# A convolution with max pooling: row sums with one operand in PSUM, head casts on ScalarE, and a new instruction order

## Chip, core and metric

One Trainium2 chip; the kernel runs on one of its cores. The metric is the device time of one execution in microseconds, the lower the better. The five engines of the core are called as in the profile: PE (TensorE; PEld is its loading of weights), DVE (VectorE), ACT (ScalarE), POOL (GpSimd) and SP (SyncE, which only issues transfers here).

## What is computed

```python
def setup_inputs():
    batch, c_in, h, w, c_out, k = 16, 64, 64, 64, 128, 3
    ...
def reference(x, weight, pool_size):          # pool_size is 2
    x_pad = np.pad(x, ((0, 0), (0, 0), (1, 1), (1, 1)))
    conv[b, co] += weight[co, ci, kh, kw] * x_pad[b, ci, kh:kh+h, kw:kw+w]   # over ci, kh, kw
    output[b, c, i, j] = np.max(conv[b, c, 2*i:2*i+2, 2*j:2*j+2])
```

A 3x3 convolution of 16 images with 64 channels into 128 channels, and the maximum over squares of 2x2. All arrays are float32 in memory; the kernel multiplies in bfloat16.

## The kernel before

Two images lie on the 128 partitions, 64 channels each (half 0 and half 1). Each of the 8 pairs of images is cut into 4 chunks of 16 image rows, so there are 32 pieces, numbered 0 to 31. A piece gives 8 rows of pooled output for each half. A matmul uses 64 rows of the PE array, and the matmuls of half 0 and half 1 run side by side: the function `product` puts the products of each half into a queue of its own (`lanes`) and issues them one from each queue at a time, three taps each, so six matmuls.

The two conv rows that are pooled together share their middle filter row. The kernel therefore computes two accumulators in PSUM for each piece and half (ta and tb), takes their maximum, and adds the common part afterwards. There are two ways to do this, told apart by the letter in `TYPES`:

- K pieces (11 of them) come from `kx`, an array already in bfloat16 (loaded by POOL's queue with a cast on the way, `LK.n.part`; the first two chunks are loaded in float32 and cast by an engine). Products PA1 and PA2 fill ta, PB1 and PB2 fill tb. `EV` (ACT) copies ta to SBUF, `MX` (DVE) takes the maximum into tb, `KS` (DVE) makes the sum of neighbouring rows, PR adds its product to tb, `OD` (ACT) copies the odd columns to SBUF, `CM` (DVE) takes the maximum with the even columns.
- W pieces (21) come from `wx`, three float32 buffers loaded by SP's queue (`L` and `LB`). `E` is the difference of neighbouring rows (on POOL, or on DVE for those in `DIFF_ON_VECTOR`), `D` the difference of rows two apart (POOL), `WS` the sum of neighbouring rows (DVE; for those in `SUM_BY_REDUCTION` as a reduction with one input, else as an addition with two inputs in SBUF). P2 makes ta from E, `SE` (ACT) copies ta into tb, P0 and P3 add the products of D to ta and tb, then EV, MX, P1 (from WS), OD and CM as above.

`MX.s.h` is the maximum of piece s and half h, and so on for all names. The head turns the weights: `g0`, `g1`, `g2` cast filter rows to bfloat16, `D0`, `D2`, `GM`, `GP` combine them (with `GS` on POOL), `T..` transposes on PE, `V..` copies the result to SBUF. `XEa`, `XEb`, `XOa`, `XOb` cast the first chunk (even and odd rows, parts a and b; tile `kfirst`), `X1` and `X2` the second (`ksecond`). `F.k.part` and `G.k.part` are the first K and W pieces' products in halves; `Ea`, `Eb`, `Da`, `Db`, `SEa`, `SEb` the first W piece's other work in halves.

Everything runs in the sequence of the text `ORDER`: each engine takes its own entries in that sequence, waiting for data and for buffers. PSUM has eight banks, handed out from a queue of free ones. One further wait is put in by hand: an operation of POOL waits for the last DVE operation, before it in the text, that was marked with `on_vector` (`on_gpsimd`, `behind`); reductions are not marked. The loads `LB` and the first `LK` wait in the same way. The output of a piece is stored by SP's queue as soon as its second CM stands in the text.

The profile's lines: 200 the products, 301 KS, 315 and 323 the two forms of WS, 332 E, 341 D, 399 and 401 EV, 411 SE, 427 MX, 431 OD, 437 CM, 353 and 368 the first W piece's E and D, 451 the casts of the first chunk, 458 of the second, 175 to 181 the weight copies, 95, 106 and 447 the transfers of kx, wx and the output.

Of the kernel before, what the change touches and what calls it, by code (L numbers as in the profile page):

```python
# [11 lines left out]
def kernel(  # L12
# [169 lines left out]

# [145 lines left out]
    def we(s):  # L328
        row["we", s] = e_pool.tile([128, R, W], BF16, name="we")
        t, f = wx_rows(s)  # L330
        vector = s in DIFF_ON_VECTOR
        inst = (nc.vector if vector else nc.gpsimd).tensor_tensor(  # L332
# [261 lines left out]
```

## Time and profile before

| | |
|---|---|
| time, median of 3 runs | 104.88 us (104.57 to 104.96) |
| profiled execution, span from first to last instruction | 103.4 us |
| the profiled execution's own time | not listed apart; the median lies 1.5 us above the span |
| busy: PE, DVE, ACT, POOL | 96.6, 91.9, 82.1, 75.7 us |
| mean granted clock of TensorE | 0.997 |
| moved by DMA | 23.33 MB, mean 226 GB/s |

All times of events are microseconds from the start of the span. A row of the timeline or of the chain gives start, duration and what ran; a group row gives line, engine, operation, output<-input, count, then busy time, mean ns of one, and the idle time just before with what ended it. The rows of stretches give the sum, then busy time (and count) of PE, PEld, DVE, ACT and POOL, the granted clock, the DMA share and GB/s. PE counts as busy from the first to the last of overlapping matmuls, so a short hole between two matmuls is seen in their starts only.

### The profile page before, as it was taken

What the parts mean: (1) busy time and instruction counts of PE and PEld (TensorE: products, weight loads), DVE (VectorE), ACT (ScalarE), POOL (GpSimd) and SP (SyncE); (2) the same over time, 40 slices, a digit from 0 to 9 for tenths busy, and PEclk for the clock granted to TensorE, in tenths of its full rate; (3) what the DMA queues carried; (4) which work ended last, traced back from release to release, by engine and by line L of the source; (5) the groups of instructions that cost most, each with busy time, mean ns of one, the idle gap of its engine ahead of it and who ended that gap; (6) DMA issues with size and microseconds to landing.
All of it is one profiled execution on the core that took longest, in us unless ns stands there. A gap on an engine that the chain in (4) does not pass through costs nothing.

```text
span 103.4 us, 2542 instructions
## 1 busy us (share of the span) xinstructions
PE 96.6 (93%) x909; PEld 60.1 (58%) x909; DVE 91.9 (89%) x179; ACT 82.1 (79%) x181; POOL 75.7 (73%) x65
## 2 busy tenths in 40 slices
...
GB/s 63 265 297 283 389 319 337 384 405 270 219 212 307 304 302 292 341 356 225 175 131 210 252 381 263 51 203 271 173 158 257 80 136 101 0 13 223 74 202 102
DMA packets 13341, 23.33 MB, mean 226 GB/s; under 512 B 1040, under 2 KB 9488, under 8 KB 13328
## 3 DMA queue, kind: packets, MB, share of 16 engines
...
q0 software_dynamic: 864, 2.36, 13.9%
q8 instruction: 7, 0.11, 0.4%
...
## 4 chain that ended last, share of the span: by engine, by line
PE 83%; DMA 6%; DVE 5%; SPq 1%; issue 1%; DVEq 0%
PE acc L200 83%; DMA wx<-in_x_dram 6%; DVE acc L427 2%; DVE o L437 2%; DVE we L353 1%; SPq L114 0%; SPq L113 0%; SPq L109 0%; DVE ks L301 0%; DVEq L589 0%; DVEq L437 0%
## 5 line engine op out<-in xcount | busy, mean ns | idle before, releaser
L200 PEld LDWEIGHTS <-wt 64*128 64x128 bf16 x876 | 57.7, 94 | 34.1 <-issue 1.6
L341 POOL TENSOR_TENSOR wd<-wx 128x1024 bf16<-128x1024 f32 x20 | 47.1, 2360 | 7.6 <-PE acc L200 2.9
L200 PE MATMUL acc<-kx,wt 64*128 64x504 bf16 (+6 forms) x288 | 50.1, 356 | 0.4 <-DVE wt L181 0.4
L200 PE MATMUL acc<-wd,wt 64*128 64x504 bf16 (+3 forms) x264 | 50.1, 367 | 0.0
L427 DVE TENSOR_TENSOR acc<-acc,ev 128x512 f32<-128x512 f32 x64 | 42.0, 693 | 0.9 <-ACT ev L401 0.3
L200 PE MATMUL acc<-we,wt 64*128 64x512 bf16 (+2 forms) x132 | 31.9, 367 | 0.0
L200 PE MATMUL acc<-ws,wt 64*128 64x504 bf16 (+1 forms) x126 | 28.7, 377 | 0.1
L401 ACT ACTIVATE ev<-acc 128x512 f32<-128x512 f32 x42 | 25.1, 608 | 2.7 <-PE acc L200 2.3
L431 ACT COPY od<-acc 128x256 f32<-128x256 f32 x64 | 22.6, 379 | 5.8 <-PE acc L200 5.2
L437 DVE TENSOR_TENSOR o<-acc,od 128x256 f32<-128x256 f32 x64 | 24.5, 416 | 2.1 <-ACT od L431 1.9
L411 ACT COPY acc<-acc 128x512 f32<-128x512 f32 x40 | 23.0, 581 | 3.0 <-PE acc L200 1.7
L332 POOL TENSOR_TENSOR we<-wx 128x512 bf16<-128x512 f32 x16 | 20.2, 1271 | 3.4 <-DVE ws L323 2.4
L200 PE MATMUL acc<-ks,wt 64*128 64x504 bf16 (+1 forms) x66 | 16.5, 377 | 0.4 <-DVE acc L427 0.4
L315 DVE TENSOR_REDUCE ws<-wx 128x512 bf16<-128x1024 f32 x11 | 13.5, 1230 | 0.0
L399 ACT COPY ev<-acc 128x512 f32<-128x512 f32 x22 | 12.9, 595 | 0.6 <-PE acc L200 0.5
L323 DVE TENSOR_TENSOR ws<-wx 128x512 bf16<-128x512 f32 x10 | 7.0, 720 | 0.0
L301 DVE TENSOR_TENSOR ks<-kx 128x512 bf16<-128x512 bf16 x11 | 4.6, 429 | 0.4 <-ACT kx L458 0.4
L551 PE MATMUL acc<-const-bfloat16-1.0 128*128 128x512 bf16 x8 | 3.3, 589 | 0.8 <-PEq L575 0.8
L95 POOL DMA_DIRECT2D kx<-in_x_dram x6 | 3.5, 587 | 0.7 <-DVE kx L451 0.7
L151 POOL COPY wq<-wq 128x64 bf16<-128x64 bf16 x3 | 0.9, 314 | 3.2 <-ACT wq L462 2.5
L465 DVE TENSOR_TENSOR wq<-wraw 128x192 bf16<-128x192 f32 x1 | 0.5, 498 | 2.6 <-DMA wraw<-in_weight_dram 2.6
L368 POOL TENSOR_TENSOR wd<-wx 128x512 bf16<-128x512 f32 x2 | 2.5, 1260 | 0.4 <-DVE we L353 0.4
...
## 6 DMA issues: line engine op xcount, KB each, us to landing
...
kx<-in_x_dram POOLq DMA_DIRECT2D x1, 496.0 KB, 13.1
```

The lines of the kernel that those rows point to most:

```text
L200: nc.tensor.matmul(acc[t][:, i0:i1, o0:o1], wt[lo : lo + CI, tap_of(m0, kw, h), :], rows(lo, i0, i1, c0, c1), start=start and kw == 1, sto ...
L301: nc.vector.tensor_tensor(out=row["ks", s], in0=t[:, f : f + 2 * R : 2, :], in1=t[:, f + 1 : f + 2 * R : 2, :], op=ADD)
L315: nc.vector.tensor_reduce(out=row["ws", s], in_=t[:, f : f + 2 * R, :].rearrange("p (r two) w -> p r w two", two=2), axis=mybir.AxisListTy ...
L323: nc.vector.tensor_tensor(out=row["ws", s], in0=t[:, f : f + 2 * R : 2, :], in1=t[:, f + 1 : f + 2 * R : 2, :], op=ADD)
L332: inst = (nc.vector if vector else nc.gpsimd).tensor_tensor(out=row["we", s], in0=t[:, f : f + 2 * R : 2, :], in1=t[:, f + 1 : f + 2 * R : ...
L341: nc.gpsimd.tensor_tensor(out=row["wd", s], in0=t[:, f + 1 : f + 1 + 2 * R, :], in1=t[:, f - 1 : f - 1 + 2 * R, :], op=SUB)
L399: nc.scalar.copy(out=ev[s, h], in_=acc[t])
L401: nc.scalar.mul(ev[s, h], acc[t], -1.0)
L411: nc.scalar.copy(out=acc[t], in_=acc[ta[s, h]])
L427: nc.vector.tensor_tensor(out=t, in0=t, in1=ev[s, h], op=MAX)
L431: nc.scalar.copy(out=od[s, h], in_=acc[tb[s, h]][:, :, 1::2])
L437: nc.vector.tensor_tensor(out=ot[s][:, h], in0=acc[t][:, :, 0::2], in1=od[s, h], op=MAX)
```

## The change

- Six row sums (pieces 4, 6, 16, 17, 19, 23) take their odd rows from a PSUM bank, into which ACT copies them first (new entry `XC`); the difference of piece 6, on DVE, reads the same copy. These DVE operations are not marked `on_vector`.
- Seven sums instead of eleven are reductions: 1, 3, 8, 11, 12, 25 and 30.
- The differences on DVE are those of 3, 6, 11 and 27 instead of 3, 4, 6 and 11.
- In the head ACT casts XEa, XOa and XOb (DVE did), DVE casts g0 (ACT did); the weight copies of G2 and G1 are on ACT and the others on DVE (G0, G2 and GM were on ACT).
- The stores are entries of their own (`ST`) and no longer follow their second CM at once.
- Six pools get one to three more buffers.
- `ORDER` is another text. Its first and last lines are shown.

```diff
@@ -35,9 +35,15 @@
 
 
     TYPES = "KWKWWKWKWWKWWKWKWWKWWKWWWWKWWKWW"
-    DIFF_ON_VECTOR = (3, 4, 6, 11,)
+    DIFF_ON_VECTOR = (3, 6, 11, 27,)
     CAST_ON_VECTOR = ()
-    SUM_BY_REDUCTION = (1, 3, 9, 11, 12, 14, 16, 17, 19, 20, 22,)
+    SUM_BY_REDUCTION = (1, 3, 8, 11, 12, 25, 30,)
+    ODD_ROWS_IN_PSUM = (4, 6, 16, 17, 19, 23,)
+    TURNED_BY_SCALAR = ("G2", "G1",)
+    CAST_BY_SCALAR = ("XEa", "XOa", "XOb",)
+    TAPS_BY_VECTOR = ("g0",)
+    SUMS_BY_GPSIMD = ()
+    COLMAX_ON_GPSIMD = ()
     N = len(TYPES)
     KSTEPS = [s for s in range(N) if TYPES[s] == "K"]
     WSTEPS = [s for s in range(N) if TYPES[s] == "W"]
@@ -47,13 +53,13 @@
 
     const = ctx.enter_context(tc.tile_pool(name="const", bufs=1))
     kx_pool = ctx.enter_context(tc.tile_pool(name="kx_pool", bufs=-(-NK // NQ)))
-    d_pool = ctx.enter_context(tc.tile_pool(name="d_pool", bufs=5))
-    e_pool = ctx.enter_context(tc.tile_pool(name="e_pool", bufs=5))
-    ws_pool = ctx.enter_context(tc.tile_pool(name="ws_pool", bufs=5))
+    d_pool = ctx.enter_context(tc.tile_pool(name="d_pool", bufs=8))
+    e_pool = ctx.enter_context(tc.tile_pool(name="e_pool", bufs=7))
+    ws_pool = ctx.enter_context(tc.tile_pool(name="ws_pool", bufs=7))
     ks_pool = ctx.enter_context(tc.tile_pool(name="ks_pool", bufs=4))
-    ev_pool = ctx.enter_context(tc.tile_pool(name="ev_pool", bufs=7))
-    od_pool = ctx.enter_context(tc.tile_pool(name="od_pool", bufs=6))
-    o_pool = ctx.enter_context(tc.tile_pool(name="o_pool", bufs=6))
+    ev_pool = ctx.enter_context(tc.tile_pool(name="ev_pool", bufs=8))
+    od_pool = ctx.enter_context(tc.tile_pool(name="od_pool", bufs=8))
+    o_pool = ctx.enter_context(tc.tile_pool(name="o_pool", bufs=8))
     psum = ctx.enter_context(tc.tile_pool(name="psum", bufs=1, space=bass.MemoryType.PSUM))
 
     ctx.enter_context(tc.manual_schedule())
@@ -171,14 +177,27 @@
         free.append(turned[m])
         lo, hi, src = turned_cols(m)
         dst = wt[:, lo:hi, :].rearrange("p a b -> p (a b)")
-        if m == "GM":
-            nc.scalar.mul(dst, src, 0.5)
-        elif m == "GP":
+        if m in TURNED_BY_SCALAR:
+            if m in ("GM", "GP"):
+                nc.scalar.mul(dst, src, 0.5)
+            else:
+                nc.scalar.copy(out=dst, in_=src)
+        elif m in ("GM", "GP"):
             nc.vector.tensor_scalar_mul(out=dst, in0=src, scalar1=0.5)
-        elif m in ("G0", "G2"):
-            nc.scalar.copy(out=dst, in_=src)
         else:
             nc.vector.tensor_copy(out=dst, in_=src)
+
+    def tap_cast(n, m, src):
+        if n in TAPS_BY_VECTOR:
+            on_vector(nc.vector.tensor_copy(out=slots(m), in_=src))
+        else:
+            nc.scalar.copy(out=slots(m), in_=src)
+
+    def tap_sum(n, m, op):
+        if n in SUMS_BY_GPSIMD:
+            on_gpsimd(nc.gpsimd.tensor_tensor(out=slots(m), in0=gsum, in1=g1, op=op))
+        else:
+            on_vector(nc.vector.tensor_tensor(out=slots(m), in0=gsum, in1=g1, op=op))
 
     def tap_of(m0, kw, half):
         if m0 in (GM, G1, GP):
@@ -307,9 +326,27 @@
         p, q = place[s]
         return wx[p % NWX], 2 * R * q + 1
 
+    copied, users = {}, {}
+
+    def odd_rows(s):
+        t, f = wx_rows(s)
+        copied[s] = free.popleft()
+        users[s] = 2 if s in DIFF_ON_VECTOR else 1
+        nc.scalar.copy(out=acc[copied[s]], in_=t[:, f + 1 : f + 2 * R : 2, :])
+
+    def with_odd_rows(s, out, op):
+        t, f = wx_rows(s)
+        nc.vector.tensor_tensor(out=out, in0=t[:, f : f + 2 * R : 2, :], in1=acc[copied[s]], op=op)
+        users[s] -= 1
+        if users[s] == 0:
+            free.append(copied[s])
+
     def ws(s):
         row["ws", s] = ws_pool.tile([128, R, W], BF16, name="ws")
         t, f = wx_rows(s)
+        if s in ODD_ROWS_IN_PSUM:
+            with_odd_rows(s, row["ws", s], ADD)
+            return
         if s in SUM_BY_REDUCTION:
             with nc.allow_low_precision("bf16 operand of TensorE, as the other row sums"):
                 nc.vector.tensor_reduce(
@@ -329,6 +366,9 @@
         row["we", s] = e_pool.tile([128, R, W], BF16, name="we")
         t, f = wx_rows(s)
         vector = s in DIFF_ON_VECTOR
+        if vector and s in ODD_ROWS_IN_PSUM:
+            with_odd_rows(s, row["we", s], SUB)
+            return
         inst = (nc.vector if vector else nc.gpsimd).tensor_tensor(
             out=row["we", s], in0=t[:, f : f + 2 * R : 2, :], in1=t[:, f + 1 : f + 2 * R : 2, :], op=SUB
         )
@@ -390,7 +430,7 @@
     def late_load(s):
         behind(wload(s), sbuf_op[0])
 
-    ev, od, ot, made = {}, {}, {}, {}
+    ev, od, ot = {}, {}, {}
 
     def evac(s, h):
         ev[s, h] = ev_pool.tile([128, R, W], FP32, name="ev")
@@ -436,19 +476,22 @@
         t = tb.pop((s, h))
         nc.vector.tensor_tensor(out=ot[s][:, h], in0=acc[t][:, :, 0::2], in1=od[s, h], op=MAX)
         free.append(t)
-        made[s] = made.get(s, 0) + 1
+
+    def store(s, h=None):
         p, q = place[s]
         dst = out[2 * p : 2 * p + 2, :, q * R : (q + 1) * R, :].rearrange("b c h w -> c b (h w)")
         src = ot[s].rearrange("p b h w -> p b (h w)")
-        if s == N - 1:
-            store = nc.scalar if made[s] == 1 else nc.sync
-            store.dma_start(out=dst[:, h : h + 1], in_=src[:, h : h + 1])
-        elif made[s] == 2:
+        if h is None:
             nc.sync.dma_start(out=dst, in_=src)
-
-
-    def cast_rows(lo, hi):
-        on_vector(nc.vector.tensor_copy(out=kx[0][:, lo:hi:2, :], in_=kfirst[:, lo:hi:2, :]))
+        else:
+            (nc.scalar, nc.sync)[h].dma_start(out=dst[:, h : h + 1], in_=src[:, h : h + 1])
+
+
+    def cast_rows(n, lo, hi):
+        if n in CAST_BY_SCALAR:
+            nc.scalar.copy(out=kx[0][:, lo:hi:2, :], in_=kfirst[:, lo:hi:2, :])
+        else:
+            on_vector(nc.vector.tensor_copy(out=kx[0][:, lo:hi:2, :], in_=kfirst[:, lo:hi:2, :]))
 
     def cast_more(first):
         dst, src = kx[0][:, klo2 + first : khi2 : 2, :], ksecond[:, first::2, :]
@@ -458,18 +501,18 @@
             nc.scalar.copy(out=dst, in_=src)
 
     steps = {
-        "g0": lambda: nc.scalar.copy(out=slots(G0), in_=g0),
-        "g1": lambda: nc.scalar.copy(out=slots(G1), in_=g1),
-        "g2": lambda: nc.scalar.copy(out=slots(G2), in_=g2),
+        "g0": lambda: tap_cast("g0", G0, g0),
+        "g1": lambda: tap_cast("g1", G1, g1),
+        "g2": lambda: tap_cast("g2", G2, g2),
         "D2": lambda: on_vector(nc.vector.tensor_sub(out=slots(D2), in0=g2, in1=g1)),
         "D0": lambda: on_vector(nc.vector.tensor_sub(out=slots(D0), in0=g0, in1=g1)),
         "GS": lambda: on_gpsimd(nc.gpsimd.tensor_tensor(out=gsum, in0=g0, in1=g2, op=ADD)),
-        "GM": lambda: on_vector(nc.vector.tensor_sub(out=slots(GM), in0=gsum, in1=g1)),
-        "GP": lambda: on_vector(nc.vector.tensor_add(out=slots(GP), in0=gsum, in1=g1)),
-        "XOa": lambda: cast_rows(1, kmid),
-        "XOb": lambda: cast_rows(kmid, khi),
-        "XEa": lambda: cast_rows(0, kmid),
-        "XEb": lambda: cast_rows(kmid + 1, khi),
+        "GM": lambda: tap_sum("GM", GM, SUB),
+        "GP": lambda: tap_sum("GP", GP, ADD),
+        "XOa": lambda: cast_rows("XOa", 1, kmid),
+        "XOb": lambda: cast_rows("XOb", kmid, khi),
+        "XEa": lambda: cast_rows("XEa", 0, kmid),
+        "XEb": lambda: cast_rows("XEb", kmid + 1, khi),
         "X1": lambda: cast_more(0),
         "X2": lambda: cast_more(1),
         "F": first_product,
@@ -482,6 +525,7 @@
         "SEb": lambda h: seed_half(1, h),
         "KS": ks, "WS": ws, "E": we, "D": wd, "L": wload, "LB": late_load, "LK": lk,
         "SE": seed, "EV": evac, "MX": rowmax, "OD": odd, "CM": colmax,
+        "XC": odd_rows, "ST": store,
     }
     for m in BLOCKS:
         steps["u" + m] = lambda m=m: ring(m)
@@ -491,59 +535,59 @@
         steps[m] = lambda s, h, m=m: product(m, s, h)
 
     ORDER = """
-        D0 g2 g1 TD0 TG2 g0 D2 XEa LB.3 LB.4 PR.0.1 TD2 VG2 PA1.2.1 VD0 TG0 uG1 TG1 GS F.2.0 VD2 XOa LB.6
-        LB.8 LB.9 GM VG0 F.3.0 XOb F.0.0 uGM F.1.0 VG1 F.0.1 TGM PA2.2.1 XEb LK.0.0 F.1.1 F.2.1 F.3.1 VGM GP
-        Ea KS.0 Eb EV.0.1 G.0.0 EV.0.0 G.0.1 uGP P2.3.1 SEa.0 SEa.1 SEb.1 MX.0.1 Da Db TGP SEb.0 MX.0.0 VGP
-        LK.0.1 X2 PR.0.0 G.1.0 X1 G.2.0 PB1.2.1 PB2.2.1 WS.1 G.2.1 G.1.1 L.11 P0.3.1 PA1.2.0 PA2.2.0 P3.3.1
-        OD.0.0 OD.0.1 EV.1.0 KS.2 E.3 CM.0.1 EV.1.1 P1.1.1 D.3 CM.0.0 PR.2.1 PB1.2.0 P2.3.0 MX.1.0 PB2.2.0
-        EV.2.1 P1.3.1 SE.3.1 EV.2.0 WS.3 MX.1.1 P1.1.0 SE.3.0 P0.3.0 MX.2.0 MX.2.1 EV.3.1 PR.2.0 EV.3.0 D.4
-        MX.3.1 OD.2.0 PA1.5.1 OD.1.0 E.4 PA1.5.0 PA2.5.0 P3.3.0 OD.1.1 OD.2.1 L.12 L.14 PA2.5.1 OD.3.1
-        P2.4.1 CM.1.1 CM.2.0 P2.4.0 CM.1.0 PA1.7.1 D.6 EV.5.0 CM.3.1 CM.2.1 MX.3.0 PA2.7.1 PB1.5.1 SE.4.0
-        PA1.7.0 PA2.7.0 EV.5.1 SE.4.1 EV.7.0 PB2.5.1 P0.4.1 P0.4.0 P2.6.1 KS.7 E.6 P3.4.1 WS.4 WS.6 P1.3.0
...
-        EV.29.0 PA2.29.1 P1.28.1 P2.30.0 EV.29.1 MX.26.1 OD.28.1 OD.27.0 PR.26.1 P1.28.0 OD.26.1 CM.26.0
-        MX.28.0 SE.30.0 CM.28.1 PB1.29.0 P0.30.0 P2.30.1 PB1.29.1 PB2.29.1 CM.26.1 CM.27.0 P0.30.1 SE.30.1
-        P2.31.0 KS.29 OD.28.0 P3.30.0 CM.28.0 P2.31.1 EV.30.0 P3.30.1 SE.31.0 PB2.29.0 PR.29.1 MX.29.1 WS.31
-        EV.30.1 P0.31.0 SE.31.1 MX.30.0 MX.29.0 EV.31.0 P0.31.1 P3.31.1 P3.31.0 PR.29.0 MX.30.1 MX.31.0
-        EV.31.1 P1.30.1 OD.29.1 P1.30.0 MX.31.1 OD.29.0 P1.31.1 CM.29.0 CM.29.1 P1.31.0 OD.30.1 CM.30.1
-        OD.30.0 OD.31.0 OD.31.1 CM.30.0 CM.31.0 CM.31.1
+        g1 g2 D2 g0 D0 uG1 TD2 XOa VD2 TG0 TG2 XEa TD0 VG2 VG0 TG1 GS VD0 GM LB.3 uGM F.0.0 F.1.0 F.2.0 LB.4 XEb
+        XOb GP F.3.0 F.0.1 LB.6 KS.0 TGM F.1.1 uGP EV.0.0 F.2.1 EV.0.1 LK.0.0 Ea VG1 VGM Eb F.3.1 MX.0.0 G.0.0
+        MX.0.1 G.0.1 WS.1 TGP SEa.0 SEb.0 SEa.1 PR.0.0 Da PR.0.1 SEb.1 G.1.0 X2 G.2.0 Db G.1.1 LK.0.1 VGP X1
+        OD.0.0 OD.0.1 E.3 G.2.1 EV.1.1 PA1.2.1 KS.2 CM.0.0 EV.1.0 PA1.2.0 CM.0.1 PA2.2.0 PA2.2.1 MX.1.1 P2.3.1
+        L.11 MX.1.0 WS.3 P1.1.1 P2.3.0 PB1.2.1 EV.2.0 PB1.2.0 PB2.2.0 EV.2.1 PB2.2.1 D.3 P1.1.0 SE.3.0 OD.1.1
+        SE.3.1 P3.3.0 CM.1.1 MX.2.0 P0.3.1 P0.3.0 PR.2.0 MX.2.1 PA1.7.0 P3.3.1 OD.1.0 E.4 EV.3.1 LB.8 CM.1.0 D.6
+        PA2.7.0 MX.3.1 PR.2.1 PA1.5.1 P1.3.1 EV.3.0 OD.2.0 MX.3.0 OD.2.1 PA2.5.1 XC.4 LB.9 CM.2.1 P1.3.0 PA1.5.0
+        CM.2.0 D.4 E.8 PB1.5.0 OD.3.1 E.9 PA2.5.0 OD.3.0 P2.4.1 WS.4 PA1.7.1 CM.3.1 EV.5.1 PA2.7.1 CM.3.0 SE.4.1
+        XC.6 P0.4.1 WS.8 P2.4.0 EV.7.0 E.6 P3.4.1 EV.5.0 WS.6 KS.7 PB1.5.1 L.16 PB2.5.0 LK.1.0 KS.5 PB1.7.0
...
+        L.24 CM.15.1 PA2.21.0 ST.10 L.31 OD.13.0 P2.20.1 CM.13.0 D.19 OD.16.1 PA1.21.1 OD.15.0 EV.17.1 ST.9
+        CM.16.1 CM.15.0 P2.19.0 MX.17.1 SE.17.0 SE.20.1 WS.24 PA2.21.1 EV.21.0 ST.12 SE.19.0 P1.17.1 P0.20.1
+        P0.17.0 KS.21 P3.20.1 EV.17.0 KS.26 P2.19.1 OD.17.1 WS.20 EV.21.1 KS.18 P3.17.0 EV.20.1 P0.19.0 MX.17.0
...
+        CM.28.0 PB1.29.1 EV.30.0 SE.30.1 PB2.29.1 EV.29.1 EV.29.0 P3.30.0 SE.31.0 PB1.29.0 P0.30.1 P2.31.1
+        EV.30.1 WS.30 D.31 MX.29.1 PR.29.1 P3.30.1 SE.31.1 PB2.29.0 ST.19 ST.15 ST.18 P0.31.0 OD.29.1 MX.30.0
+        EV.31.0 ST.26 WS.31 P0.31.1 P3.31.0 MX.29.0 EV.31.1 P3.31.1 PR.29.0 CM.29.1 MX.30.1 P1.30.1 ST.27
+        OD.29.0 MX.31.0 P1.30.0 OD.30.0 ST.28 P1.31.0 MX.31.1 CM.29.0 CM.30.0 OD.30.1 P1.31.1 ST.29 OD.31.0
+        CM.30.1 OD.31.1 CM.31.0 ST.30 ST.31.0 CM.31.1 ST.31.1
```

More of the change, by code (lines that the diff above doesn't have):

```diff
@@ new lines @@
+        MX.6.0 CM.6.1 P1.6.0 SE.9.1 L.20 P0.8.1 CM.7.1 OD.6.0 P3.8.1 MX.8.0 P2.9.0 P2.11.0 L.14 EV.8.1 P1.8.0
+        P0.9.1 CM.6.0 P3.9.1 MX.8.1 SE.9.0 P1.8.1 PA1.10.1 D.11 EV.9.1 OD.8.0 PA2.10.1 E.14 WS.9 P3.9.0 CM.8.0
+        P0.9.0 PA1.13.0 OD.8.1 L.19 PA2.13.0 D.14 SE.11.0 MX.9.1 ST.0 P0.11.0 CM.8.1 ST.2 EV.9.0 EV.10.1 P1.9.1
+        MX.9.0 P2.11.1 PA1.13.1 KS.10 P1.9.0 P3.11.0 OD.9.1 EV.13.0 CM.9.1 KS.13 SE.11.1 WS.14 PA2.13.1 LK.1.1
+        D.12 P0.11.1 OD.9.0 P2.14.0 L.17 PA1.10.0 PA2.10.0 EV.11.0 P3.11.1 CM.9.0 EV.13.1 P2.12.1 SE.14.0
@@ new lines @@
+        PB1.10.1 EV.11.1 D.16 WS.11 E.16 ST.8 P0.14.0 MX.11.0 P2.12.0 EV.10.0 PB2.10.1 SE.12.1 EV.14.0 SE.12.0
+        P1.11.0 MX.11.1 WS.12 P3.14.0 P1.11.1 P0.12.1 E.17 OD.11.0 P0.12.0 P3.12.1 P3.12.0 EV.12.1 ST.6 ST.4
+        MX.10.1 PB1.10.0 OD.11.1 CM.11.0 EV.12.0 LK.2.0 MX.14.0 PB2.10.0 P1.14.0 PR.10.1 MX.12.1 OD.10.1 P2.14.1
+        CM.11.1 P1.12.1 CM.10.1 XC.17 MX.12.0 MX.10.0 ST.3 PB1.13.1 P1.12.0 PB2.13.1 SE.14.1 OD.12.1 PR.10.0
+        P0.14.1 OD.14.0 CM.12.1 ST.7 PA1.15.0 D.17 CM.14.0 L.23 MX.13.1 OD.12.0 PA2.15.0 P3.14.1 CM.12.0 OD.10.0
@@ new lines @@
+        CM.10.0 PR.13.1 E.20 EV.14.1 MX.14.1 XC.16 PA1.15.1 OD.13.1 P1.14.1 CM.13.1 EV.15.0 P2.16.0 PA2.15.1
+        PB1.13.0 P2.16.1 PB1.15.1 SE.16.0 OD.14.1 WS.16 PB2.13.0 WS.17 PA1.18.0 CM.14.1 EV.15.1 E.22 PB2.15.1
+        KS.15 WS.22 LK.2.1 P0.16.0 SE.16.1 MX.13.0 PA2.18.0 MX.15.1 P0.16.1 EV.16.0 P3.16.0 MX.16.0 EV.16.1
+        P3.16.1 ST.5 P2.17.1 PB1.15.0 PR.15.1 PB2.15.0 P1.16.0 EV.18.0 MX.16.1 P1.16.1 E.19 MX.15.0 PR.13.0
+        XC.19 SE.17.1 OD.16.0 P0.17.1 D.20 L.25 ST.14 WS.19 P3.17.1 PR.15.0 P2.17.0 OD.15.1 PA1.21.0 CM.16.0
```

59 lines of the change are left out of this document (21 added, 38 removed).

## The prediction

> **What bounds the kernel now.** I read the page's busy shares first (PE 93%, DVE 89%, ACT 79%, POOL 73%), then the chain that ended last in order of time, because shares do not tell where the end is set.
>
> ```profile
> 8.59 0.42 DVE we L353
> ...
> 9.65 1.30 DVE acc L427 x2
> 10.95 0.04 issue
> 10.99 64.95 PE acc L200 x609
> 75.94 0.02 issue
> 75.96 20.42 PE acc L200 x186
> 96.38 0.03 issue
> 96.41 0.66 DVE acc L427
> ...
> 97.73 1.74 DVE o L437 x5
> ```
>
> From 10.99 on the chain is one run of matmuls: PE is the path for 85 us, until VectorE (DVE) closes it. What can be won lies before 10.99, in small holes of the PE run, and after 96.4. Six matmuls (three taps on both halves) start every 0.645 us (the rows of the PE timeline at 18.24 and 18.89 are three taps apart). I call such a six a step and number them: step 0 is the PR.0 pair at 10.99, step 1 the first kx pair at 13.02 (four half products lie between), step 131 the last P1 pair. Steps come from the order text by pairing the entries of half 0 and half 1 one to one, as `product` does. 130 steps of 0.645 from 13.02 reach 96.87; step 131 started at 97.87, so the holes are 1.0 us in all. Starts that lie too far apart in the PE timeline place 0.25 at 75.5, 0.14 at 78.3, some 0.2 in six small ones and 0.4 at 97.4.
>
> The second view is the table of stretches (sum of the stretch, then PE, PEld, DVE, ACT, POOL busy).
>
> ```profile
> 20.00:35.00 15.00, 15.00 (x142) 9.24 (x140) 14.84 (x31) 12.53 (x30) 11.68 (x8) 1.00 1.01 291
> 35.00:50.00 15.00, 15.00 (x142) 9.44 (x140) 15.00 (x27) 12.17 (x28) 14.07 (x10) 1.00 0.98 293
> 65.00:80.00 15.00, 14.98 (x140) 8.57 (x138) 14.38 (x29) 13.56 (x30) 12.95 (x9) 1.00 0.76 191
> ```
>
> DVE is as full as PE from 20 to 65 us, but it is just in time: it makes no hole there. The holes at 75 and 78 come behind it and behind ACT (ScalarE).
>
> **The row sums.** The groups give the prices.
>
> ```profile
> L427 DVE TENSOR_TENSOR acc<-acc,ev 128x512 f32<-128x512 f32 x64 | 42.0, 693 | 0.9 <-ACT ev L401 0.3 <-DVE acc L427 0.2
> L411 ACT COPY acc<-acc 128x512 f32<-128x512 f32 x40 | 23.0, 581 | 3.0 <-PE acc L200 1.7 <-DVE o L437 0.4
> L315 DVE TENSOR_REDUCE ws<-wx 128x512 bf16<-128x1024 f32 x11 | 13.5, 1230 | 0.0
> L323 DVE TENSOR_TENSOR ws<-wx 128x512 bf16<-128x512 f32 x10 | 7.0, 720 | 0.0
> ```
>
> Sums now: 11 x 1.230 + 10 x 0.720 = 20.7 us of DVE. After: 7 reductions, 6 sums with one operand in PSUM, 8 with both in SBUF. No row shows the PSUM form; between the 0.720 of L323 and the 0.693 of L427, which also has one operand in PSUM, I take 0.693. Sum: 8.6 + 4.2 + 5.8 = 18.5, so 2.2 less. The Trainium skill (Perfetto Trace Analysis, Optimizing Scalar/DVE Operations) speaks against this: it puts the access overhead of DVE at about 60 ns on SBUF and 125 on PSUM; by that, an estimate, the six sums would cost 0.4 us more than the SBUF form. The rows hardly show it: back to back, L427 starts every 0.63 us (four in 2.51 from 16.08) and L323 every 0.60.
>
> What the SBUF form costs beyond its row is a wait for GpSimd (POOL):
>
> ```profile
> 72.01 2.35 POOL L341 TENSOR_TENSOR wd<-wx 128x1024 bf16<-128x1024 f32 x1
> 74.07 0.84 DVE L323 TENSOR_TENSOR ws<-wx 128x512 bf16<-128x512 f32 x1
> 67.79 1.27 POOL L332 TENSOR_TENSOR we<-wx 128x512 bf16<-128x512 f32 x1 [0.51 <-DVE ks L301]
> 68.74 0.87 DVE L323 TENSOR_TENSOR ws<-wx 128x512 bf16<-128x512 f32 x1
> ```
>
> Both sums began before the POOL operation ended (74.36, 69.06) and took 0.16 and 0.18 us more than the 0.68 of the undisturbed ones; reductions over POOL work stay at 1.22 to 1.26. The Trainium skill (SBUF — State Buffer, Who interferes with whom) has it that a DVE instruction with two SBUF inputs and a GpSimd one that reads SBUF exclude each other, and the later blocks fully. The trace agrees: those sums end about 0.6 us after POOL does.
>
> The gain of 2.2 us is off the path except where DVE makes a hole: at 75 and 78 us, 0.4 in all. That is the credit I give; at most all 1.0.
>
> **The other side of the sums.** ACT gets six copies of 512 from SBUF to PSUM: between 0.581 (L411) and the 0.630 of the cast from ksecond, 3.5 to 3.8 us. It takes three head casts (some 0.36 each, the 256-wide copy), gives up one weight copy (1.6 to 1.1) and g0 (0.5): 82.1 becomes 85.7. Behind each copy wait the EV, SE and OD of its stretch, and behind those PE. Following ACT's queue to step 35 at its spacing (EV and SE 0.5, OD 0.33) I find it at PE's heels but not late: SE.4.0 ends 0.1 before P0.4.0 needs it. From 0 to 0.6; I take 0.1. A bank is also held from the copy to the sum, out of eight: the next taker waits 0 to 0.2 (P2.6.1 for EV.4.1), within that 0.1.
>
> **The head.** First half products now start at 6.22. DVE loses three casts and ACT gets them: D2, TD2, VD2 are done at 5.4, and XOa, waiting for kfirst (5.46), at 5.9, so the first product starts near 5.95. This gain dies at the next wait: Ea cannot start before wx lands at 8.57. Then VGM, which was on ACT and done by 8.9, stands behind Ea on DVE (0.34): G.0.0 goes from 9.26 to 9.4, Eb and both MX.0 follow, and step 0 from 10.99 to 11.1: +0.1 (bounds -0.2, if Ea is 0.1 early, and +0.3). The loads LB.3 and LB.4 are issued behind GM, near 6.6 and not 5.86; ksecond ahead of them lands at 11.07 in the same queue, so they land as before.
>
> **The order.** Most entries stay within two steps of their place. One does not: PA1.7.0 goes from step 13 to step 10. It reads kx rows 49 to 63, the load LK.0.1 on POOL's queue, which stays behind Db:
>
> ```profile
> 12.26 0.57 POOL L95 DMA_DIRECT2D kx<-in_x_dram  x1
> ```
>
> ```profile
> kx<-in_x_dram POOLq DMA_DIRECT2D x1, 240.0 KB, 7.6
> ```
>
> 12.26 + 7.6 = 19.86 is the landing. Step 13 came at 13.02 + 12 x 0.645 = 20.8: covered by 0.9. Step 10 would come at 13.02 + 0.1 + 9 x 0.645 = 18.9. Da and Db stand ahead of LK.0.1 as before, so its issue stays at 12.3. LK.0.0, ahead on the same queue, is issued at 7.75 and not 8.28, and two wx loads (8, 9) are now queued later, behind KS.2, so fewer bytes compete: 19.3 at the earliest, 20.2 with nothing gained. PE would stand 0.4 to 1.3 us at step 10; I take 0.7. PE runs in order, so all steps behind it move.
>
> The stores become entries of their own (ST) and stand later in SP's queue; the pools grow (d 8, e 7, ws 7, ev 8, od 8, o 8), which only takes waits away. Where an o slot is tightest, CM.28 at step 119 needs what ST.23 frees; ST.23 follows ST.24, which waits for CM.24.1 at step 106, and lands 4.7 us (seven steps) later (the median of section 6): covered by five steps. L.28, behind ST.17 (CM.17.0, step 81), lands some 8 us later, step 94; E.28 is wanted by P2.28.1 at 109. Cost 0; without these covers one CM or one E waits for a landing, 1 to 3 us.
>
> In the middle the new order meets POOL anew; DVE's SBUF sums, the KS and the E on DVE can each wait for up to one POOL operation (1.27 or 2.36). The 25 such instructions of now lost some 0.4 together; I take +0.2 (0 to 1.2).
>
> **The tail.** WS.30 becomes a reduction (1.23) just ahead of MX.29.1, and CM.29.1 goes ahead of MX.30.1. From the start of step 121, with 0.65 for an MX, 0.6 for a sum and 0.35 for a CM, DVE is at CM.28.0 by 0.85, WS.30 2.0, MX.29.1 2.65, MX.30.0 3.4, WS.31 4.0, MX.29.0 4.65, CM.29.1 5.0, MX.30.1 5.6, MX.31.0 6.2, MX.31.1 6.8; step 131 wants that at 6.45 and waits 0.4, as it does now (MX.31.1 ended at 97.8, 6.8 after step 121). Five CM in place of six follow, set by OD.31.1. So 0, from -0.4 to +0.4. Stores ST.15, 18, 19 and 22, held back, go out behind CM.25.0 some 8 us before the end, in a stretch with a DMA share of 0.33; the last store lands 2.4 us after its issue as now.
>
> **Sum.** +0.1 head, +0.7 step 10, +0.1 ACT and banks, -0.4 old holes, +0.2 POOL, 0 tail: +0.7. The profiled span is 103.4, 1.5 under the median of 104.88; 104.1 of span, 105.6 as a time.
>
> **Rivals.** *Faster:* LK.0.1 lands by 19, and DVE, lighter by 2.4 us in all (2.2, plus 1.0 of casts, less 0.4 each for copies and g0), is early at every old hole: 0.4 in the middle and 0.4 at the end are gone and 0.1 is lost in the head. 104.2. For it: 2 of 7 loads less in front. Against: 240 KB at the two queues' shared rate took 3.3 us behind LK.0.0, which the trace has landing at 16.54. *No change:* the wait at step 10 is real and pays for the holes, +0.1 +0.7 -0.8: 104.9. *Lock:* a wd of 2.36 us begins just before a DVE sum with slack below a step. The place is the group KS.21, KS.26, WS.20, KS.18 and WS.24 at steps 73 to 75, with D.20 and D.19 back to back on POOL (4.7 us) and MX.17.0 due at step 78; it decides if D.19 starts before WS.24. Loss 2.36 less some 1.0 of slack, and again once elsewhere: 2.7 on an otherwise even sum, less the 0.4: 107.2.
>
> **How the numbers follow.** The measurement can tell 0.5%, so 104.36 to 105.40 is no change. Forecast 105.6 with 0.35 (its own range 105.4 to 106.4), lock 0.12: slower 0.47. No change 0.25, faster 0.28. The range 103.9 to 106.8 leaves out the lock and the best of the faster case, under 0.2.
>
> **What would show it.** Right: a PE hole before a kx pair near 19 us, released by the kx load; no hole at DVE near 75; DVE some 2.4 us less busy, ACT 3.6 more; PSUM-fed sums near 0.69; first products near 5.95 but step 0 near 11.1. Wrong: LK.0.1 landing by 18.9, PSUM-fed sums at 0.8 or more, ACT as releaser of PE's holes, or a PE run of 85 us or less between step 0 and the end.

## The result and the profile after

The changed kernel takes 106.43 us (median of 6 runs, 105.84 to 107.94), the kernel before, run beside it, 104.83 us (104.32 to 105.28): ratio 1.0135, 95% interval 1.0097 to 1.0174. It is 1.4% slower. (A ratio here compares undisturbed executions alone, so it can differ from the quotient of the medians.) The profiled execution took 105.84 us, with a span of 104.1 us.

The busy shares say little: PE, DVE and POOL are where they were, ACT has 3.0 us more.

```profile
PE 97.4 (94%) x910; PEld 60.3 (58%) x910; DVE 91.8 (88%) x178; ACT 85.1 (82%) x188; POOL 75.6 (73%) x65
```

The chain that ended last, in order of time (start, duration, what), has a new link.

```profile
8.96 2.40 POOL wd L408 x2
11.35 0.04 issue
11.39 7.82 DMA kx<-in_x_dram
19.22 0.04 issue
19.26 43.40 PE acc L219 x400
...
62.76 0.62 DVE acc L467
63.37 0.04 issue
63.42 32.24 PE acc L219 x294
```

Before, the chain was one run of matmuls from 10.99 to 96.4. Now PE's work before 19.2 is off the chain: the kx load LK.0.1, issued at 11.39 behind Da and Db, lands at 19.22, and step 10 starts at 19.26. In the timeline the wait stands at its place (in square brackets: how long the engine stood idle, and what ended it):

```profile
18.34 0.65 ACT L471 COPY od<-acc 128x256 f32<-128x256 f32 x2
18.87 0.61 ACT L335 COPY acc<-wx 128x512 f32<-128x512 f32 x1
19.05 0.75 DVE L477 TENSOR_TENSOR o<-acc,od 128x256 f32<-128x256 f32 x2
19.26 1.02 PE L219 MATMUL acc<-kx,wt 64*128 64x512 bf16 x7 [0.87 <-DMA kx<-in_x_dram]
```

The last matmul before started at 17.92; with the usual 0.21 between starts this is a hole of 1.13 us (the 0.87 counts from the modelled end of that matmul). Step 1 started at 12.30, so step 10 was due at 12.30 + 9 x 0.645 = 18.1.

A second hole of 0.32 stands at step 78, where MX.17.0 waits in DVE's queue. DVE had lost 0.62 ahead of it on a load:

```profile
60.45 0.69 DVE L360 TENSOR_TENSOR ws<-wx 128x512 bf16<-128x512 f32 x1 [0.62 <-DMA wx<-in_x_dram]
61.06 0.75 DVE L320 TENSOR_TENSOR ks<-kx 128x512 bf16<-128x512 bf16 x2
61.73 0.68 DVE L360 TENSOR_TENSOR ws<-wx 128x512 bf16<-128x512 f32 x1
62.34 0.42 DVE L320 TENSOR_TENSOR ks<-kx 128x512 bf16<-128x512 bf16 x1
62.67 0.69 DVE L467 TENSOR_TENSOR acc<-acc,ev 128x512 f32<-128x512 f32 x1
```

The first is WS.24, which waits for chunk 24; then KS.21, KS.26, WS.20, KS.18 and MX.17.0, as the order has them. Further holes in the starts of PE: 0.25 at 76.7, 0.11 at 78.3, 0.12 at 86.6 and 0.45 at 97.9 (step 131). The table of stretches shows PE full again outside these places (columns as before):

```profile
20.00:35.00 15.00, 15.00 (x144) 9.50 (x142) 13.56 (x27) 12.94 (x29) 12.84 (x9) 1.00 0.99 316
50.00:65.00 15.00, 14.87 (x140) 8.12 (x138) 14.19 (x30) 13.74 (x30) 11.36 (x8) 1.00 0.91 261
65.00:80.00 15.00, 15.00 (x141) 8.45 (x138) 14.38 (x27) 13.28 (x31) 14.28 (x9) 1.00 0.45 143
```

The groups of the row sums (line, engine, operation, count, then busy us, mean ns, idle time before):

```profile
L352 DVE TENSOR_REDUCE ws<-wx 128x512 bf16<-128x1024 f32 x7 | 8.6, 1227 | 0.0
L360 DVE TENSOR_TENSOR ws<-wx 128x512 bf16<-128x512 f32 x8 | 5.7, 725 | 0.6 <-DMA wx<-in_x_dram 0.6
L339 DVE TENSOR_TENSOR ws<-wx,acc 128x512 bf16<-128x512 f32 x6 | 4.0, 680 | 0.0
L335 ACT COPY acc<-wx 128x512 f32<-128x512 f32 x6 | 3.6, 603 | 0.0
```

**A measure for comparing profiles.** The head ends at another time in every execution: step 1 started between 12.40 and 13.02 in six profiles with the head of before, and between 12.30 and 12.88 in six with the changed head. The means, 12.61 and 12.63, are the same. So I compare the stretch from step 1 to the start of the last matmul: 85.3 us before (98.30 - 13.02), 86.65 after (98.95 - 12.30). The 1.35 us between them is nearly the whole of the 1.4% by time. Where PE waits for a landing, though, the stretch depends on how that landing lies to step 1. In the five profiles below and here with the changed head and LK.0.1 behind the same loads (three of them without a wait, since they read those rows later) it came 6.1 to 6.9 us after step 1. Less nine steps, 5.8, the hole at step 10 would be 0.3 to 1.1 us, an estimate; this execution has the longest.

### The profile page after: what moved, and what is told of

Read it like the earlier page. It is cut to its first block, busy times and chain, and to the rows that moved or that the text cites. A ratio compares the mean times of both kernels' runs of the same rounds, so it can differ in the third digit from the quotient of the medians.

```text
span 104.1 us, 2529 instructions
## 1 busy us (share of the span) xinstructions
PE 97.4 (94%) x910; PEld 60.3 (58%) x910; DVE 91.8 (88%) x178; ACT 85.1 (82%) x188; POOL 75.6 (73%) x65
## 4 chain that ended last, share of the span: by engine, by line
PE 73%; DMA 10%; DVE 6%; POOL 3%; issue 2%; DVEq 0%; ACT 0%; POOLq 0%
PE acc L219 73%; DMA kx<-in_x_dram 8%; DMA wraw<-in_weight_dram 3%; POOL wd L408 2%; DVE acc L467 2%; DVE wt L188 1%; DVE wq L200 1%; DVE o L477 1%; POOL kx L101 1%; DVE wq L507 0%; DVE wq L508 0%; DVE wq L192 0%; ACT od L471 0%; POOL wq L157 0%; DVEq L633 0%
## 5 line engine op out<-in xcount | busy, mean ns | idle before, releaser
L219 PE MATMUL acc<-kx,wt 64*128 64x504 bf16 (+6 forms) x288 | 48.0, 356 | 0.9 <-DMA kx<-in_x_dram 0.9
L219 PE MATMUL acc<-we,wt 64*128 64x512 bf16 (+3 forms) x132 | 30.8, 367 | 0.0
L219 PE MATMUL acc<-ws,wt 64*128 64x504 bf16 (+1 forms) x126 | 29.7, 377 | 0.3 <-DVE acc L467 0.2
L477 DVE TENSOR_TENSOR o<-acc,od 128x256 f32<-128x256 f32 x64 | 25.1, 418 | 2.8 <-ACT od L471 2.1
L219 PE MATMUL acc<-ks,wt 64*128 64x504 bf16 (+1 forms) x66 | 15.5, 377 | 0.0
L352 DVE TENSOR_REDUCE ws<-wx 128x512 bf16<-128x1024 f32 x7 | 8.6, 1227 | 0.0
L360 DVE TENSOR_TENSOR ws<-wx 128x512 bf16<-128x512 f32 x8 | 5.7, 725 | 0.6 <-DMA wx<-in_x_dram 0.6
L320 DVE TENSOR_TENSOR ks<-kx 128x512 bf16<-128x512 bf16 x11 | 5.1, 477 | 0.0
L339 DVE TENSOR_TENSOR ws<-wx,acc 128x512 bf16<-128x512 f32 x6 | 4.0, 680 | 0.0
L335 ACT COPY acc<-wx 128x512 f32<-128x512 f32 x6 | 3.6, 603 | 0.0
```

Of the source, the lines that this page charges most:

```text
L219: nc.tensor.matmul(acc[t][:, i0:i1, o0:o1], wt[lo : lo + CI, tap_of(m0, kw, h), :], rows(lo, i0, i1, c0, c1), start=start and kw == 1, sto ...
L320: nc.vector.tensor_tensor(out=row["ks", s], in0=t[:, f : f + 2 * R : 2, :], in1=t[:, f + 1 : f + 2 * R : 2, :], op=ADD)
L352: nc.vector.tensor_reduce(out=row["ws", s], in_=t[:, f : f + 2 * R, :].rearrange("p (r two) w -> p r w two", two=2), axis=mybir.AxisListTy ...
L360: nc.vector.tensor_tensor(out=row["ws", s], in0=t[:, f : f + 2 * R : 2, :], in1=t[:, f + 1 : f + 2 * R : 2, :], op=ADD)
L477: nc.vector.tensor_tensor(out=ot[s][:, h], in0=acc[t][:, :, 0::2], in1=od[s, h], op=MAX)
```

## The experiments

My theory: the wait for LK.0.1 at step 10 is what makes the kernel slower; head, sums and the rest of the order cancel. Its rivals: the order as a whole or ACT's extra work is slower, and the wait only takes up time that was lost anyway; or the sums and the head cost by themselves. All ratios are to the kernel before in the same comparison.

**The kernel before, once more**, unchanged, for the scatter.

> The kernel before, unchanged, to see how much two profiles and two sets of times of one program differ. In the changed kernel kfirst landed at 4.38 and the first wx part at 7.14, before at 5.46 and 8.57, though the transfers issued up to then are the same. If this is chance from run to run, the landings here differ from 5.46 and 8.57 by up to 1.4 us and step 1 from 13.02 by up to 0.7; if it is the new head, they are within 0.2. Time within 0.5% of before either way.

104.76 against 104.76 us, ratio 0.9996 (0.9972 to 1.0021). kfirst landed at 4.69, the first wx part at 6.69, and step 1 came at 12.41. With nothing changed the wx landing moved by 1.9 us, more than the 1.4 that I had allowed to chance, so these early landings need no new head. Step 1 to the last matmul 85.3 us. Differences below 0.3% are not told apart here.

**The changed kernel with pieces 5 and 7 exchanged** (their PA and EV of half 0), so that rows 49 to 63 are read at step 13 again:

```diff
-  ... MX.2.1 PA1.7.0 P3.3.1 ... PA2.7.0 ... PA1.5.0 ... PA2.5.0 ... EV.7.0 ... EV.5.0
+  ... MX.2.1 PA1.5.0 P3.3.1 ... PA2.5.0 ... PA1.7.0 ... PA2.7.0 ... EV.5.0 ... EV.7.0
```

> The changed kernel with PA1, PA2 and EV of pieces 5 and 7, half 0, in each other's places, so that kx rows 49 to 63 are first read at step 13 and not 10. Theory (wait for the kx load): the hole of 1.1 us before step 10 is gone, the time falls by 0.8 to 1.2 us, to 1.002 to 1.006 of before. Rival (DVE and POOL set the pace there and the hole only stands where they would make one a few steps later): it falls by less than 0.4 us.

Ratio 1.0016 (0.9975 to 1.0057). The load landed as late as ever, at 19.40, and nobody waited for it; the chain is one run of matmuls from the head to 92.8:

```profile
11.66 81.11 PE acc L219 x761
```

Step 1 to the last matmul: 85.2 us, as before. The hole at step 78 was gone as well, though nothing was changed there.

**The same exchange in the kernel before**, so that the old order reads those rows at step 9.

```diff
-  ... PA1.5.0 PA2.5.0 ... PA1.7.0 PA2.7.0 ...
+  ... PA1.7.0 PA2.7.0 ... PA1.5.0 PA2.5.0 ...
```

> The kernel before with the same exchange, so that kx rows 49 to 63 are first read at step 9 and not 13. Theory (wait for the kx load): with a landing of 19.2 to 19.9 against step 9 at 18.2 a hole of 1.0 to 1.7 us opens there and the time rises by 0.9 to 1.7 us (1.009 to 1.016 of before). Rival: under 0.4 us.

Ratio 1.0112 (1.0073 to 1.0151), 86.45 us from step 1 to the last matmul, 1.15 more. The chain of this run shows the same link in a kernel with none of the change's sums, head or pools:

```profile
11.45 7.41 DMA kx<-in_x_dram
18.85 0.05 issue
18.90 57.76 PE acc L200 x529
```

So the wait can be put in and taken out by three pairs of names, worth 1.4 us one way and 1.15 the other. That is the theory, shown from both sides; the 1.4 holds the hole at step 78 too.

**The load issued earlier**: LK.0.1 ahead of Da.

```diff
-  ... PR.0.0 Da PR.0.1 SEb.1 G.1.0 X2 G.2.0 Db G.1.1 LK.0.1 VGP ...
+  ... PR.0.0 LK.0.1 Da PR.0.1 SEb.1 G.1.0 X2 G.2.0 Db G.1.1 VGP ...
```

> The changed kernel with the load LK.0.1 ahead of Da on POOL, so issued near 8.6 and not 11.4. Theory (wait for the kx load): it lands 0.5 to 2 us earlier, the hole before step 10 shrinks by as much, up to its 1.1 us; Da, Db and G.1 may come up to 0.6 us later, so the time falls by 0.3 to 1.1 us. Rival (pace of DVE and POOL): no gain, or a loss of up to 0.6 from Da.

Ratio 1.0124 (1.0064 to 1.0184). Issued 2.4 us earlier, the load landed no earlier, where I had expected 0.5 to 2 us:

```profile
8.99 10.32 DMA kx<-in_x_dram
19.31 0.04 issue
19.35 43.40 PE acc L219 x400
```

The hole was still 0.73 us (step 1 had come 0.5 later). Its place in POOL's queue is not what delays it.

**Fewer bytes ahead of it**: load L.11, which goes out at 7.89 and lands at 17.67 in the changed kernel, behind LB.9.

```diff
-  ... PA2.2.1 MX.1.1 P2.3.1 L.11 MX.1.0 ... XC.4 LB.9 CM.2.1 ...
+  ... PA2.2.1 MX.1.1 P2.3.1 MX.1.0 ... XC.4 LB.9 L.11 CM.2.1 ...
```

> The changed kernel with the load of wx chunk 11 (512 KB) behind that of chunk 9, so that it does not run beside kx rows 49 to 63. Issuing that kx load 2.4 us earlier did not make it land earlier (19.31 against 19.22). If it is held by the bytes that share the engines with it, it now lands 0.5 to 1.3 us earlier and the hole at step 10 falls from 1.1 to 0.6 us or less: time 0.4 to 1.0 us lower, 1.004 to 1.010 of before. If it is held by its own queue (the cast transfers run at some 100 KB per us whatever runs beside), landing and time stay as they are.

LK.0.1 was issued at 11.56, as late as in the changed kernel, and landed at 17.48, 1.7 us earlier. The DMA rows (KB, median us from issue to landing), the changed kernel's and then this one's:

```profile
kx<-in_x_dram POOLq DMA_DIRECT2D x1, 240.0 KB, 7.8
```

```profile
kx<-in_x_dram POOLq DMA_DIRECT2D x1, 240.0 KB, 5.9
```

No hole at step 10, 85.3 us from step 1 to the last matmul, ratio 1.0048 (1.0015 to 1.0081). In all other profiles with this order LK.0.1 landed between 18.67 and 19.40, so 17.48 is clear of their scatter: the landing goes with the bytes that the wx loads move at the same time. The hole at step 78 shrank to 0.07 here too: of the runs of this order, only the two with the wait at step 10 had it in full. It follows the wait of WS.24 for chunk 24, which was 0.62 us in those two, 0.31 here and 0.15 with the exchange: the chunk landed at 60.36 and 60.45 in those two, at 59.52 here and at 59.41 with the exchange. In those two its load had been issued some 0.5 later and took another 0.3 to 0.5 longer; why it took longer stays open. The span behind the last matmul was 0.45 longer than in the kernel before (5.56 against 5.09), since the last store landed later. That would be most of what the ratio keeps, but the run of the exchange has 5.53 there at a ratio of 1.0016, so it is not shown.

**The sums without PSUM** (on top of the exchange): no XC; sums 16, 17 and 19 as reductions, 4, 6 and 23 and the difference of 6 with both operands in SBUF.

```diff
-    SUM_BY_REDUCTION = (1, 3, 8, 11, 12, 25, 30,)
-    ODD_ROWS_IN_PSUM = (4, 6, 16, 17, 19, 23,)
+    SUM_BY_REDUCTION = (1, 3, 8, 11, 12, 16, 17, 19, 25, 30,)
+    ODD_ROWS_IN_PSUM = ()
```

> The exchange of 5 and 7, without the copies to PSUM: sums 16, 17 and 19 are reductions again, 4, 6 and 23 additions with both inputs in SBUF, as in the kernel before. If PE sets the pace and the lighter DVE buys nothing, the time is that of the exchange alone within 0.4 us, though DVE is 1.6 us busier and ACT 3.6 us less. If the lighter DVE is worth something here, it is slower by 0.5 to 1.6 us, with holes of PE released by DVE.

Ratio 1.0285 (1.0247 to 1.0323), 88.3 us from step 1 to the last matmul: 3.1 more than with the exchange alone, and more than the 0.5 to 1.6 that I had allowed. DVE, at 94.8 us of busy time (91.6 with the exchange alone), now makes most of the holes, by reductions and by what waits for POOL: the sum of piece 4 took 1.76 us in all and the difference of piece 6 1.18, where 0.68 is undisturbed. From the chain, which counts their last parts only:

```profile
19.27 0.65 DVE o L477 x2
19.92 0.92 DVE ws L360
...
23.41 0.90 DVE we L372
...
51.61 0.91 DVE ws L352
52.52 0.15 issue
52.67 1.24 DVE ws L352
...
66.24 0.61 DVE ws L360
...
66.99 1.27 POOL we L372
```

The last lines are of another kind: sums with both operands in SBUF are marked `on_vector` and the PSUM sums are not, so here POOL's difference E.23 waits for WS.23, and PE has a hole of 0.72 behind it at 67.4. In this order the PSUM sums are on the path. How much of the 3 us is DVE's time and how much the marks was not tested apart.

**Three sums from PSUM in the kernel before**: 16, 19 and 20, each XC six entries ahead of its WS, all else as before.

```diff
-    SUM_BY_REDUCTION = (1, 3, 9, 11, 12, 14, 16, 17, 19, 20, 22,)
+    SUM_BY_REDUCTION = (1, 3, 9, 11, 12, 14, 17, 22,)
+    ODD_ROWS_IN_PSUM = (16, 19, 20,)
```

> The kernel before with one part of the change alone: the sums of pieces 16, 19 and 20 take their odd rows from PSUM (an XC six entries ahead of each) where they were reductions; the order is otherwise that of before. DVE gives up 3 x 0.53 = 1.6 us, ACT gets 3 x 0.60 = 1.8. My step (a lighter DVE is worth only the holes that DVE makes): ratio 0.996 to 1.001, at best the 0.25 us hole near 75.5 gone, no other hole less. Rival A (a sum in PSUM saves about 0.9 us of path wherever it stands, as three did in the new order): 0.97 to 0.98. Rival B (the copy stands in ACT's queue ahead of an EV or SE and holds one of eight banks): new PE holes released by ACT near 55, 65 or 70 us, 0.2 to 0.5 us in all, ratio 1.002 to 1.005.

Ratio 1.0222 (1.019 to 1.0255): all three expectations missed, the third only in size. Step 1 to the last matmul took 87.6 us, 2.3 more, with holes of 0.76 at 47.5, 1.16 at 59.3 and 0.44, 0.38 near 64 and 66. Up to the first copy the two kernels run alike; then (timeline):

```profile
47.55 0.60 ACT L317 COPY acc<-wx 128x512 f32<-128x512 f32 x1
48.02 0.42 DVE L456 TENSOR_TENSOR o<-acc,od 128x256 f32<-128x256 f32 x1
48.07 0.60 ACT L420 ACTIVATE ev<-acc 128x512 f32<-128x512 f32 x1
48.35 0.68 DVE L321 TENSOR_TENSOR ws<-wx,acc 128x512 bf16<-128x512 f32 x1
48.48 0.37 PE L201 MATMUL acc<-kx,wt 64*128 64x512 bf16 x1 [0.53 <-DVE o L456]
```

The copy takes one of the eight banks; the next product gets the one that a CM frees at 48.44, and PE stands until then. Two more runs tell this from the delay in ACT's queue.

**The same three copies into SBUF**, into a tile that nobody reads, with the sums as reductions: ACT's work without the bank.

```diff
+    def odd_rows(s):
+        t, f = wx_rows(s)
+        nc.scalar.copy(out=spare, in_=t[:, f + 1 : f + 2 * R : 2, :])
```

> The kernel before with the three copies of 512 that the run with three sums in PSUM put into ACT's queue, at the same places, but into a tile of SBUF that nobody reads; the sums stay reductions. So ACT has the same 1.8 us more, no bank is held, and DVE is as before. If the 2.3 us lost there are the banks' (a copy takes one of eight, and the next taker waits for a CM to free another): at most 0.3 us slower, ratio 0.999 to 1.004, no PE hole of 0.5 near 47 or 59 us. If they are ACT's (what stands behind a copy in its queue is 0.6 late): the same holes, ratio 1.015 to 1.025.

Ratio 1.0047 (1.0014 to 1.0081), a little more than the 1.004 that I allowed the copies; 85.8 us, 0.5 more than before: no hole at 47, but 0.34 at 59.5 and 0.42 at 63.6. So ACT's queue is 0.5 of the 2.3. The rest goes with the sums' use of PSUM, at 47.5 shown as a wait for a bank.

**The three sums with each XC right ahead of its WS**: the bank is held only for the copy and the sum.

```diff
-  ... MX.10.0 OD.14.0 XC.16 P3.14.1 ... PB2.13.1 WS.16 ...
+  ... MX.10.0 OD.14.0 P3.14.1 ... PB2.13.1 XC.16 WS.16 ...
```

> The kernel before with the sums of 16, 19 and 20 from PSUM, but each XC right ahead of its sum and not six entries ahead of it: a bank is taken later and held only for the copy and the sum (1.3 us), and the sum waits for the copy on DVE. If the time that a bank is held is what costs: the holes near 47 and 59 us shrink, ratio 1.003 to 1.012. If it costs as much that the copy takes a bank out of its turn at all: 1.015 to 1.025 still. If ACT's queue is what costs: 1.015 or more, with DVE waiting for ACT's copy in front of the holes.

Ratio 1.0125 (1.009 to 1.016), 86.7 us, 1.4 more. The ratio lies between the first two ranges that I had named. The hole at 47.5 is gone, with 0.16 left at 49.0; those at 59.5 and 64.2 (0.91 and 0.68) are not gone. They now end behind a sum that frees its bank (the second one in the timeline below), and the sums wait 2.5 us for ACT's copies:

```profile
L321 DVE TENSOR_TENSOR ws<-wx,acc 128x512 bf16<-128x512 f32 x3 | 2.1, 688 | 2.5 <-ACT acc L317 2.5
```

```profile
65.09 0.37 PE L201 MATMUL acc<-kx,wt 64*128 64x512 bf16 x1 [0.45 <-DVE ws L321]
```

So when a bank is taken and given back matters. Whether taking it at all costs, or only DVE's wait for the copy, this run does not tell apart. In this order, which has no bank to spare at 47.5, the form costs more than it gives either way.

**The old head's engines in the new order** (on top of the exchange).

```diff
-    TURNED_BY_SCALAR = ("G2", "G1",)
-    CAST_BY_SCALAR = ("XEa", "XOa", "XOb",)
-    TAPS_BY_VECTOR = ("g0",)
+    TURNED_BY_SCALAR = ("G0", "G2", "GM",)
+    CAST_BY_SCALAR = ()
+    TAPS_BY_VECTOR = ()
```

> The exchange of 5 and 7, with the head's casts and weight copies on the engines that had them before (XEa, XOa, XOb on DVE, g0 on ACT, copies of G0, G2, GM on ACT). If the gain of the moved casts dies at the next wait, step 1 stays within 0.2 us of the 12.3 to 12.9 seen with the new head and the time within 0.3 us. If they help, step 1 comes 0.3 to 0.6 us later and so does the end.

Ratio 1.0231 (1.0186 to 1.0277). Step 1 came at 14.47, some 1.8 late, where I had expected 0.6 at most; from there to the last matmul it took 85.4. G.0.0 waits at 10.87 for the GM copy, which stands behind both EV.0 on ACT:

```profile
PE acc L219 <- ACT wt L182: 0.9, 1, 0.9
```

The engine choice and the order of the head belong together as well.

**Towards a faster kernel**: on top of the exchange, L.24 ahead of store ST.14, and WS.30 exchanged with KS.29 so that the reduction is out of the tail; then L.24 alone (the first pair of lines).

```diff
-  ... L.25 ST.14 WS.19 ... CM.16.0 L.24 CM.15.1 ...
+  ... L.25 L.24 ST.14 WS.19 ... CM.16.0 CM.15.1 ...
-  ... PB2.26.0 KS.29 PA1.26.1 ... EV.30.1 WS.30 D.31 ...
+  ... PB2.26.0 WS.30 PA1.26.1 ... EV.30.1 KS.29 D.31 ...
```

> The exchange of 5 and 7, the load of wx chunk 24 ahead of the store of piece 14 (it landed at 60.36, and WS.24 waited 0.6 us for it, with a hole of 0.3 at step 78 behind), and WS.30 and KS.29 in each other's places, so that the reduction of 1.23 us is no longer just ahead of the last maxima. Theory: the hole of 0.4 at step 131 and, where it shows, that of 0.3 at step 78 go: 0.3 to 0.7 us below the exchange alone, 0.995 to 0.999 of before, and less scatter. Rival (the end is set by PE, EV and P3.31 and not by DVE's queue): no difference over 0.2 us.

> The changed kernel with the exchange of pieces 5 and 7 and with load L.24 ahead of store ST.14, WS.30 and KS.29 where they were. If chunk 24 is what WS.24 and behind it step 78 wait for: no hole at 78 and 0.1 to 0.3 us less than with the exchange alone, ratio to before 0.998 to 1.001. If the exchange of WS.30 and KS.29 was harmless in the earlier run: the same as there, 1.003 to 1.006. If what is left at step 78 is DVE's own queue (KS.21, KS.26, WS.20 ahead of MX.17.0): a hole of 0.1 to 0.3 stays there, and 1.001 to 1.002.

Both: 1.0045 (1.0017 to 1.0073), with 0.55 instead of 0.39 at step 131 though WS.30 had left DVE's tail. L.24 alone: 1.0021 (0.9995 to 1.0047), which decides between none of the cases named ahead. Neither gains on the exchange alone, which has no hole at step 78 to lose. None of the runs points to a version faster than the kernel before.

## Why the prediction was right, and where it was not

The side and the mechanism were right, and 106.43 lies in the range of 103.9 to 106.8. The forecast of 105.6 was 0.8 low. Behind step 1 the profiled executions differ by 1.4 us, where the sum had 0.6: 0.3 more at step 78, where it had nothing, and 0.4 more at step 10. By its steps:

**Step 10, +0.7.** Right in mechanism, and 0.7 lies in the middle of the 0.3 to 1.1 estimated from five profiles. The profiled execution has 1.13, and removing the wait by the exchange gave 1.4, with the hole of 0.32 at step 78 that went along and that my sum did not have. The landing was 19.22, just under the 19.3 that I called the earliest, but PE was at step 10 by 18.1 and not 18.9. I had taken the time of step 1 from one execution, 13.02, the latest of those twelve; the mean is 12.6. The term is a landing less a step, and its bounds should have held the scatter of both. Both came earlier than I had them; that their difference held as well as it did is partly luck.

**The head, +0.1.** The first product at 5.77 (forecast 5.95) looks right, but the same profiles have it between 5.76 and 6.22 with the old head and between 5.77 and 6.34 with the new one, so it shows no gain. Step 0 at 10.06 and not 11.1 is wrong. I took the landing of the first wx load, 8.57, for a fixed wall. In the other profiles it landed between 6.64 and 7.76 with the same issue time. On the average of six profiles each the head costs nothing. In the changed kernel an earlier step 1 could not count: PE's work ahead of step 10 ends at the landing at 19.22. That the profiled span of 104.1 is what I forecast is luck: step 1 came 0.8 earlier, the rest took 0.8 longer than my sum had it.

**The row sums.** Sizes right: 8.6 + 5.7 + 4.0 = 18.3 us against 18.5, and 0.680 for the PSUM form against 0.693. The Trainium skill (Perfetto Trace Analysis, Optimizing Scalar/DVE Operations) has the overhead on PSUM at twice that on SBUF; the trace does not agree for this operation: the undisturbed SBUF sums take 0.68 as well. (The 0.63 between MX starts in the prediction is a misreading: the three starts behind 16.08 are 0.60 to 0.62 apart, much as those of the SBUF sums.) What fell is "off the path except where DVE makes a hole". It was argued from the slack in the order of before. In the new order the six sums are worth some 3 us, their missing marks included, and in the old order three such sums lose 2.3, of which 0.5 is ACT's queue. The term for ACT and banks, 0.1, was enough here: between the first and the last copy, 18.87 and 64.5, the changed kernel has no hole but those of the two loads. The old order shows that this is no property of the form.

**The old holes, -0.4.** Not gone: 0.25 at 76.7 and 0.11 at 78.3 stand where 0.25 and 0.14 stood. DVE was not lighter by busy time, 91.8 against 91.9, which counts instructions that overlap only once. By the durations of its instructions (count times mean of its groups) it was 1.4 us lighter and not 2.4: its sums fell by 2.2 and the first casts by 1.1 as forecast, weight copies and g0 took back 1.0, and KS (477 ns against 429) and the differences on SBUF (806 against 683) took 0.9 more; MX and CM kept their means. What lengthened the differences is the wait for POOL again, here for the one of piece 27:

```profile
67.63 2.35 POOL L381 TENSOR_TENSOR wd<-wx 128x1024 bf16<-128x1024 f32 x1
69.48 1.05 DVE L372 TENSOR_TENSOR we<-wx 128x512 bf16<-128x512 f32 x1
```

The Trainium skill (SBUF — State Buffer, Who interferes with whom) has such pairs exclude each other, and here too the DVE instruction ended some 0.55 after POOL's. Five such waits cost DVE some 1.4 us, where the prediction counted 0.4 before. The +0.2 that I had put on them is not to be seen as a hole over 0.12. So the small terms came to about nothing in all, as forecast, but by errors that cancel.

**The rivals.** *Faster* needed the load by 19, *no change* that the old holes go and pay for the wait: the load came at 19.22, PE was there a full microsecond before it, and the holes stayed. *Lock*: its place was right, its mechanism not: KS.21 to KS.18 did make the hole at step 78, but D.19 started only at 62.83, behind them. WS.24 had waited for a load that was queued behind a store.

**The tail, 0.** Right: 0.45 at step 131, 0.4 before.
